# Squares of x one pair to a step, B's rows loaded from another place, and norm's splits in two parts

## The chip, the cores and the metric

The kernel runs on one core of one Trainium2 chip. The metric is the device time of an execution in microseconds (us); a smaller time is better. Five engines work in parallel, each on a queue of its own: TensorE (PE in the profile; its weight loads are listed apart as PEld), VectorE (DVE), ScalarE (ACT), GpSimd (POOL) and SyncE (SP), which here only issues DMA transfers.

## What is computed

One inference step of a hybrid decoder layer for 256 prompt tokens and 8 x 8 sample tokens, 320 tokens in all, with a model width of 2048. Cut to what matters here:

```python
h = rms_norm(x, norm_mix_pre)
proj = h @ w_in                                   # u, v, z, (x, B, C), dt
# head group 1: gated MLP over chunks of 128 tokens
v = layer_norm(gelu(a_v))
gate_out = gelu(a_u) * (tril(w_s) @ v + b_s)
# head group 2: SSD
xbc = silu(causal_depthwise_conv(xbc))
y, state = ssd_scan(xs, softplus(dt_raw + bias), -exp(a_log), B, C, state)
y = (y + d_skip * xs) * silu(z)
y = y * rsqrt(mean(y * y, per group of 512) + EPS) * norm_w
x = x + rms_norm(concat(gate_out, y) @ w_out, norm_mix_post)
# then the feed-forward part
x = x + rms_norm(conv_ffn(rms_norm(x, norm_ffn_pre)), norm_ffn_post)
```

For the samples the SSD part keeps one state of 64 x 128 for each head and each of the 8 sequences; every new state is the old one times a decay, plus an outer product of x and B.

## The kernel before

The activations are held transposed: 128 features on the partitions, and 320 tokens in a row. All large products are made in three parts, so that they come close to fp32. Each weight slab is loaded by SP into a tile `wraw`, rounded by ACT into `whi` (line 123), and what is left over is formed by DVE as `wlo` (line 124). PE then makes hi x hi, hi x lo and lo x hi (lines 134 to 136), 128 x 128 weights by 320 tokens each. Three buffers of each of the three tiles turn over, so a load waits until the slab three places earlier has been split, and a split waits until PE has used the slab three places earlier.

**The order of the work** is fixed when the kernel is built. Each engine gets one queue; the order in it comes from priorities (mostly the order in which the program text runs, with weight slabs and the blocks marked `first()` ahead of it), and `tc.issue_after(i)` puts an instruction behind instruction `i` on the same engine. Work between the large products is written as generators: `bg` is a list that is worked off from its head, `side` a list whose members all move on. `tick()`, called between slabs, lets them advance; `yield 24, 0` says that the next step is due after 24 more matmuls.

**The first pass over v** (lines 688 to 719) is a loop over the 16 blocks `kt` of the 2048 input features. Each step splits one block of x into hi and lo (`x_ready`, with ACT's part kept in `x_split`), and multiplies 768 columns of v's weights, 18 matmuls to a step. Beside it stand `x_squares` (squares of two blocks on ACT, line 631, an addition on DVE, line 633), `dt_columns` (the weights of dt, loaded into a `wraw` buffer and scaled into `w_dt` by DVE, line 492), `dt_products`, and `root`, which sums the squares over the features by four small matmuls and makes their reciprocal root `r` with eleven small DVE operations (`rsqrt_of`). `with_r1` then spreads `r` over the partitions with three PE transposes (line 300), at the first `tick` of the next projection.

**The gate part** is a loop over four groups `g`. It projects u for the next group (`gate_up`, whose results pass through buffers `pv`, four of them, and a Gelu on ACT), mixes v for this group (`gate_mix`, loads by POOL), and multiplies by w_out (`chunk_out`).

**The SSD part** begins with copies of B by token. B was written earlier, row by row, into a DRAM tile `b_d`. For the prompt the rows are read back by POOL while the gate part runs. For the samples two tiles `b4` are loaded by SP at the begin of this part (line 856), each of them 32 rows repeated four times; `b_of_samples` (lines 858 to 863) rounds them on ACT and forms the low part of half the partitions on DVE. `ssd(g)` is a generator in `bg`: it loads states (lines 869 and 898), multiplies them with C (`yo_ps`, line 973), and then goes through 13 numbered steps, in which `shrinks`, `picks`, `ends` and `heads` say what is done when. `shrunk` multiplies a state by its decay on POOL (line 984). `heads_in` makes the convolution input of a group and `conv_proj` its convolution (DVE, line 462), `heads_out` the z projection; its `norm` (lines 1151 to 1161) is a generator in `side`: partial sums of squares, then the root and the scaling of four blocks of y (line 1160), each split into `ohi` (ACT, line 402) and `olo` (DVE, line 403) for `chunk_out`.

Of the kernel before, what the change touches and what calls it, by code (L numbers as in the profile page):

```python
# [8 lines left out]
F32 = mybir.dt.float32  # L9
# [3 lines left out]
ALU = mybir.AluOpType  # L13
# [3 lines left out]
P = 128  # L17
NP = 256
NB, TS = 8, 8
NS = NB * TS  # L20
NT = NP + NS
# [12 lines left out]
def hybrid_step(  # L34
# [10 lines left out]
    act, dve, pool, pe, sp = nc.scalar, nc.vector, nc.gpsimd, nc.tensor, nc.sync  # L45
# [6 lines left out]
    tp = ctx.enter_context(tc.tile_pool(name="tp", bufs=2))  # L52
# [46 lines left out]
    def col(i):  # L99
        return prm[:, i:i + 1]  # L100


    def first():

        return tc.high_priority(offset=200000)
# [25 lines left out]
    def accumulate(ps, w, xhi, xlo, first, last):  # L131
        whi, wlo = w
        made_so_far[0] += 3
        pe.matmul(ps, whi, xhi, start=first, stop=False)  # L134
        pe.matmul(ps, whi, xlo, start=False, stop=False)  # L135
        last_made[0] = pe.matmul(ps, wlo, xhi, start=False, stop=last).ins  # L136
        return last_made[0]

    def rows_of(w, k0, nk, c0, n):
        return w[k0 * P:(k0 + nk) * P, c0:c0 + n].rearrange("(k p) n -> p k n", p=P)  # L140
# [6 lines left out]
    def advance(tasks, task):  # L147

        try:
            need = next(task) or (0, 0)  # L150
            due[task] = made_so_far[0] + need[0], need[1]
            return True
        except StopIteration:
            tasks.remove(task)
            return False
# [13 lines left out]
    def finish(task):  # L169
        while task in side:  # L170
            advance(side, task)
        while task in bg:
            advance(bg, bg[0])
# [187 lines left out]
    b_d = dr.tile([NT, 512], F32, name="b_d")  # L361
# [34 lines left out]
    def split(hi, lo, x, scale=None):  # L396

        if scale is None:
            act.copy(hi, x)
            made = dve.tensor_tensor(out=lo, in0=x, in1=hi.bitcast(F32), op=ALU.subtract)  # L400
        else:
            high.append(act.activation(hi, x, AF.Copy, scale=scale).ins)
            made = dve.scalar_tensor_tensor(out=lo, in0=x, scalar=scale, in1=hi.bitcast(F32), op0=ALU.mult, op1=ALU.subtract)

        return made.ins
# [20 lines left out]
    def in_order(ap):  # L426

        return ap.rearrange("p (i j f) -> p j i f", j=4, f=32)
# [6 lines left out]
    with ExitStack() as mctx:  # L435
        op = mctx.enter_context(tc.tile_pool(name="op", bufs=1))
# [155 lines left out]
        with tc.tile_pool(name="gp", bufs=1) as gp:  # L592
# [21 lines left out]
            x_split = []  # L614
# [13 lines left out]
            def x_squares(kt):  # L628

                sq = acc[:, kt:kt + 2, :]  # L630
                act.activation(sq, xf[:, kt:kt + 2, :], AF.Square)
                if kt:
                    dve.tensor_tensor(out=acc[:, 0:2, :], in0=acc[:, 0:2, :], in1=sq, op=ALU.add)
# [54 lines left out]
            for kt in range(KD):  # L688
                x_ready(kt, 1)
                x = [h[:, kt, :] for h in hT]  # L690
                if kt < 4:
                    for g in range(2):
                        wb = slab(rows_of(w_in, kt, 1, V0 + 384 * g, 384), g, begins=kt + g == 0)
                        if kt == 0:
                            made_so_far[0] += 9
                            for i in (0, 2, 1):
                                for j in range(3):
                                    pe.matmul(ps[3 * g + j][:, :NT], wb(0, j)[i // 2], x[i % 2], start=i == 0, stop=False)
                        else:
                            for j in range(3):  # L700
                                accumulate(ps[3 * g + j][:, :NT], wb(0, j), *x, False, False)
                else:
                    wb = slab(rows_of(w_in, kt, 1, V0, 768))
                    for j in range(6):
                        accumulate(ps[j][:, :NT], wb(0, j), *x, False, kt == KD - 1)
                if 3 <= kt < 11:
                    x_squares(2 * (kt - 3))
                if kt in (5, 8):
                    dt_columns(kt // 8)
                if kt == 12:  # L710
                    r = root()
                if kt == 13:
                    dt_products()
                if kt == 14:

                    with tc.issue_after(rounded[0]):
                        act.activation(held, ones[:, 0:1], AF.Gelu)
# [57 lines left out]
            def gate_up(g):  # L775
                uf = gp.tile([P, 4, NT], F32, tag="vf", name="uf", bufs=2)
                project(w_in, U0 + 512 * g, lambda j, ps: scaled(ps, AF.Gelu, uf[:, j, :]))
                return uf
# [52 lines left out]
            for g in range(4):  # L831
                res = []
                mix = gate_mix(g, uf, res)
                bg.append(mix)
                if g < 3:
                    uf = gate_up(g + 1)
                    finish(mix)
                    chunk_out(w_out, g, *res, g == 0)
            finish(mix)
# [3 lines left out]
        with tc.tile_pool(name="sd", bufs=1) as sd:  # L843
            btok = sd.tile([P, 2, 512], F32, name="btok")

            bsp = sd.tile([P, 2, 512], F32R, name="bsp")
# [3 lines left out]
            pool.tensor_copy(cb[NS:, NT:], ident[NS:, NS:])  # L850
            for c in range(2):
                act.copy(btok[:, c].rearrange("p (j i f) -> p j i f", j=4, f=32), in_order(b_raw[:, 512 * c:512 * c + 512]))
            b4 = [sd.tile([P, 512], F32, tag=tag, name="b4", bufs=n) for tag, n in (("s1", 1), ("xde", 2))]
            for i in range(2):
                o = NP + 32 * i
                sp.dma_start(b4[i], b_d[o:o + 32].unsqueeze(0).broadcast_to([4, 32, 512]))

            def b_of_samples():
                for i in range(2):
                    act.copy(bsp[:, i].rearrange("p (j i f) -> p j i f", j=4, f=32), in_order(b4[i]))  # L860
                    for rs in (slice(32, 64), slice(96, P)):
                        h = bsp[rs, i].rearrange("p (j i f) -> p j i f", j=4, f=32)
                        dve.tensor_tensor(out=h, in0=in_order(b4[i][rs]), in1=h.bitcast(F32), op=ALU.subtract)

            def load_state(g, i):

# [13 lines left out]
            def ssd(g):  # L880
# [63 lines left out]
                for r in range(2):  # L944
# [3 lines left out]
                                  in0=ps[:, :NP].rearrange("p (c t) -> p c t", c=2),  # L948
                                  in1=upper.unsqueeze(1).to_broadcast([P, 2, P]), op=ALU.mult)
                dve.tensor_tensor(out=cb[NS:, :NS], in0=ps[NS:, NP:NT], in1=upper_s[NS:], op=ALU.mult)  # L950
                dve.tensor_tensor(out=cb[:NS, NT:], in0=ps[:NS, NP:NT], in1=upper_s[:NS], op=ALU.mult)
                for hb in range(2):
                    dve.tensor_tensor(out=cms[:, 4 * hb:4 * hb + 4], in0=cmask[:, 4 * hb:4 * hb + 4],
                                      in1=cT[:, g, NP + 32 * hb:NP + 32 * hb + 32].unsqueeze(1).to_broadcast([P, 4, 32]),
                                      op=ALU.mult)
# [60 lines left out]
                s1 = sd.tile([P, 512], F32, tag="s1", name="s1", bufs=1)  # L1016
# [49 lines left out]
                                             op0=ALU.mult, op1=ALU.add)  # L1066
                ends = {2: 0, 5: 1, 7: 2, 10: 3}
                picks = {0: (0, 1), 2: (2,), 5: (3,)}
                shrinks = {0: 0, 3: 1, 5: 2, 8: 3}
                e = 1 if g == 3 else 0  # L1070
                heads = {0: 0, 1: 1, 3: 2, 4: 3, 5: 4, 7: 5, 9 - e: 6, 10 - e: 7}
                states = {4: (g, 3), 7: (g + 1, 0), 9: (g + 1, 1), 12: (g + 1, 2)}
# [1 line left out]
                for n in range(13 - e):  # L1074
# [23 lines left out]
                    if n < 12 - e:  # L1098
# [4 lines left out]
                                   in1=dec[:, 2, h0:h0 + 8].unsqueeze(2).to_broadcast([P, 8, 64]), op=ALU.mult)  # L1103
# [19 lines left out]
            def final(g):  # L1123
# [7 lines left out]
                yield  # L1131

            tasks = [ssd(g) for g in range(4)]
            res = [[] for _ in range(4)]

            def heads_out(g):

                ssq = hp.tile([P, NT], F32, tag="ssq", name="ssq")
                y = x_of.pop(g)

                def z_evac(j, ps):
                    while y_made.get(g, -1) < j:
                        advance(bg, bg[0])
                    zs = tp.tile([P, NT], F32, tag="ev", name="zs", bufs=2)
                    with first():
                        scaled(ps, AF.Silu, zs)
                        dve.tensor_tensor(out=y[:, j, :], in0=y[:, j, :], in1=zs, op=ALU.mult)
                        add_square(ssq, y[:, j, :], j == 0, dve)
                project(w_in, Z0 + 512 * g, z_evac)

                def norm():
                    yield 24, 0
                    small = partial_sums(ssq, ssq_d[g])
                    yield 24, 0
                    rb = tp.tile([P, NT], F32, tag="pv", name="rb", bufs=4)
                    root_by_vector(small, ssq_d[g], 1.0 / 512, rb)

                    res[g] += [h[:, KD - 4:] for h in hT] if g == 3 else out_parts(hp, "o")
                    for j in range(4):
                        dve.tensor_tensor(out=y[:, j, :], in0=y[:, j, :], in1=rb, op=ALU.mult)  # L1160
                        split(res[g][0][:, j, :], res[g][1][:, j, :], y[:, j, :], col(prm_at["norm"][3] + 4 * g + j))
                task = norm()
                side.append(task)
                return task
# [97 lines left out]
    with tc.tile_pool(name="fp", bufs=1) as fp:  # L1262
# [157 lines left out]
        for k in BY_POOL:  # L1420
            f = acc[:, k, :]
# [111 lines left out]
```

## Time and profile before

| | us |
|---|---|
| median of 3 runs | 1766.85 |
| the three runs | 1763.17, 1766.85, 2859.62 |
| profiled execution | 1763.86 |
| its span | 1762.2 |

The span is divided by the profile into busy and idle time of each engine. A line of a timeline gives the start in us, the duration in us, the engine, the line of the kernel, the operation, the tiles written and read, their shapes and a count; in brackets stands how long the engine was idle before it, and what ended that. A line of a table by stretches gives the busy time of PE, PEld, DVE, ACT and POOL in the stretch with the number of instructions that began in it, then the granted clock of TensorE, the share of DMA time and GB/s. A line of waits says who waited for whom, in total, how often, and at most. Times of matmuls are modelled at their end.

| part | about us in the span |
|---|---|
| first pass over v | 5 to 54 |
| rest of v, B, C and the first heads, gate part | 54 to 424 |
| SSD part with its projections | 424 to 810 |
| feed-forward part | 812 to 1747 |

### The profile page before, as it was taken

The page shows a single profiled execution, that of the slowest core. Times are in us where ns is not written, and L with a number is a line of the kernel's source. Part 1 is how long each engine was busy: PE and PEld are TensorE (multiplying, and loading weights), DVE is VectorE, ACT ScalarE, POOL GpSimd, SP SyncE. Part 2 cuts the span into 40 slices and gives each one's busy share as a digit, 9 for nine tenths or more (in the row PEclk, how much of TensorE's full clock was granted, in tenths as well). Part 3 has the DMA queues.
Part 4 walks back from the last instruction along what each step waited for, and adds up shares of the span by engine and source line. Part 5 has one row for each costly group of instructions (what it writes and reads, how often), then busy time and mean ns, then how long its engine had stood idle before and what let it go on. Part 6 is the DMA issues. An engine that isn't in the chain of part 4 may idle for free.

```text
span 1762.2 us, 31244 instructions
## 1 busy us (share of the span) xinstructions
PE 1751.7 (99%) x12129; PEld 1730.0 (98%) x12129; DVE 1170.2 (66%) x2000; ACT 826.8 (47%) x1216; POOL 321.8 (18%) x683
## 2 busy tenths in 40 slices
PE   9999999999999999999999999999999999999998
PEld 9999999999999999999999999999999999999998
DVE  6548863656869787788855565665657565656575
ACT  6344545333656575645545434343434343333445
POOL 2432330000314323012211101010202010101004
PEclk9999999999999999999999999999999999999999
DMA  7786654445676766665654444545454545454542
GB/s 238 225 239 185 181 175 151 151 154 151 221 217 190 226 213 201 208 207 164 178 154 153 150 153 151 154 149 154 149 155 148 155 148 152 151 155 146 155 150 105
DMA packets 228796, 302.25 MB, mean 172 GB/s; under 512 B 20904, under 2 KB 153896, under 8 KB 228456
## 3 DMA queue, kind: packets, MB, share of 16 engines
q1 hardware_dynamic: 213752, 274.61, 51.4%
q0 software_dynamic: 5312, 12.26, 2.3%
q10 hardware_dynamic: 9584, 13.38, 2.1%
q8 instruction: 96, 1.57, 0.4%
q14 instruction: 52, 0.43, 0.1%
HBM read 280.51 MB, written 19.69 MB: 170 GB/s over the span
## 4 chain that ended last, share of the span: by engine, by line
PE 90%; DVE 4%; DMA 3%; issue 1%; ACT 1%; POOL 1%; SPq 0%; ACTq 0%; POOLq 0%; DVEq 0%
PE ps L134 18%; PE ps L135 18%; PE ps L136 18%; PE pd L134 10%; PE pd L135 10%; PE pd L136 10%; DVE wlo L124 1%; DMA wraw<-in_w_in 1%; PE y_ps L1054 1%; DMA st<-in_state_ssm 1%; DMA wraw<-in_ffn_w_up 1%; ACT whi L123 0%; PE sg L801 0%; PE up_ps L990 0%; POOL st L984 0%
## 5 line engine op out<-in xcount | busy, mean ns | idle before, releaser
L124 DVE TENSOR_TENSOR wlo<-wraw,whi 128x1024 fp32r<-128x1024 f32 (+2 forms) x480 | 581.9, 1213 | 420.6 <-ACT whi L123 418.7
L123 ACT CAST whi<-wraw 128x1024 fp32r<-128x1024 f32 (+2 forms) x479 | 495.7, 1035 | 664.3 <-PE ps L135 376.6
L134 PE MATMUL ps<-h_hi,whi 128*128 128x320 f32 x2428 | 751.0, 310 | 0.9 <-ACT whi L123 0.8
L136 PE MATMUL ps<-h_hi,wlo 128*128 128x320 f32 x2428 | 748.6, 309 | 0.7 <-DVE wlo L124 0.7
L135 PE MATMUL ps<-h_lo,whi 128*128 128x320 f32 x2428 | 749.1, 309 | 0.0
L134 PEld LDWEIGHTS ps<-h_hi,whi 128*128 128x128 f32 x2428 | 456.2, 188 | 4.2 <-issue 1.2
L136 PEld LDWEIGHTS ps<-h_hi,wlo 128*128 128x128 f32 x2428 | 456.3, 188 | 1.0 <-DVE wlo L124 1.0
L135 PEld LDWEIGHTS ps<-h_lo,whi 128*128 128x128 f32 x2428 | 456.5, 188 | 0.4
L136 PE MATMUL pd<-fhi,wlo 128*128 128x320 f32 x704 | 217.0, 308 | 0.0
L134 PE MATMUL pd<-fhi,whi 128*128 128x320 f32 x704 | 217.0, 308 | 0.0
L135 PE MATMUL pd<-flo,whi 128*128 128x320 f32 x704 | 217.0, 308 | 0.0
L134 PE MATMUL pd<-ohi,whi 128*128 128x320 f32 x448 | 138.9, 310 | 0.5 <-DVE pad L456 0.5
L136 PE MATMUL pd<-ohi,wlo 128*128 128x320 f32 x448 | 138.3, 309 | 0.0
L135 PE MATMUL pd<-olo,whi 128*128 128x320 f32 x448 | 138.3, 309 | 0.0
L134 PEld LDWEIGHTS pd<-fhi,whi 128*128 128x128 f32 x704 | 132.2, 188 | 0.0
L135 PEld LDWEIGHTS pd<-flo,whi 128*128 128x128 f32 x704 | 132.2, 188 | 0.0
L136 PEld LDWEIGHTS pd<-fhi,wlo 128*128 128x128 f32 x704 | 132.2, 188 | 0.0
L1298 POOL COPY ptf<-pad 128x2 f32<-128x2 f32 x88 | 21.1, 240 | 599.5 <-DVE pad L1286 599.0
L247 DVE TENSOR_TENSOR acc_ffn<-acc_ffn,pd 128x320 f32<-128x320 f32 (+1 forms) x161 | 77.4, 481 | 37.7 <-PE pd L136 36.3
L134 PEld LDWEIGHTS pd<-ohi,whi 128*128 128x128 f32 x448 | 84.1, 188 | 1.6 <-PE pd L136 0.9
L135 PEld LDWEIGHTS pd<-olo,whi 128*128 128x128 f32 x448 | 84.1, 188 | 0.3
L136 PEld LDWEIGHTS pd<-ohi,wlo 128*128 128x128 f32 x448 | 84.1, 188 | 0.0
(338 smaller groups left out, 1751.3 us busy)
## 6 DMA issues: line engine op xcount, KB each, us to landing
wraw<-in_ffn_w_up SPq DMA_DIRECT2D x176, 512.0 KB, 3.6
wraw<-in_w_in SPq DMA_DIRECT2D x132, 512.0 KB, 3.8
wraw<-in_ffn_w_down SPq DMA_DIRECT2D x88, 512.0 KB, 3.3
wraw<-in_w_out SPq DMA_DIRECT2D x64, 512.0 KB, 3.4
st<-in_state_ssm SPq DMA_DIRECT2D x40, 256.0 KB, 4.6
out_ssm_state_sample<-st ACTq DMA_DIRECT2D x30, 256.0 KB, 3.1
cs<-dacs_d SPq DMA_DIRECT2D x16, 320.0 KB, 5.0
wraw<-in_w_in SPq DMA_DIRECT2D x12, 384.0 KB, 4.0
```

Of the source, the lines that this page charges most:

```text
L123: rounded[:] = [act.copy(hi, raw).ins]
L124: dve.tensor_tensor(out=lo, in0=raw, in1=hi.bitcast(F32), op=ALU.subtract)
L134: pe.matmul(ps, whi, xhi, start=first, stop=False)
L135: pe.matmul(ps, whi, xlo, start=False, stop=False)
L136: last_made[0] = pe.matmul(ps, wlo, xhi, start=False, stop=last).ins
L247: added_last[:] = [dve.tensor_tensor(out=acc[:, nb, ts], in0=acc[:, nb, ts], in1=ps[:, ts], op=ALU.add).ins]
L1054: pe.matmul(ps[64 * i:64 * i + 64, cols], w(hl), x(hl, m, cpx), tile_position=(0, 64 * i), **flags)
L1298: pool.tensor_copy(ptf[:, k, :], pad[:, 256:258])
```

## The change

The squares of x begin at step 6 of the first pass instead of step 3, still one pair to a step, and on ACT they are put behind the split of that step's block of x. The root moves from step 12 to step 15, the last. B's rows for the samples are loaded within the gate part's loop, when the last projection of u has been written out (`g == 2`), into the four buffers `pv`, in halves of 256 columns, by POOL; `b_of_samples` works on these halves, with four copies and eight subtractions in place of two and four. The second state of each group is shrunk at step 2 instead of 3. `norm` yields after the second of its four blocks, so that the other two are due 24 matmuls later.

```diff
-                if 3 <= kt < 11:
-                    x_squares(2 * (kt - 3))
+                if 6 <= kt < 14:
+                    with tc.issue_after(x_split[-1]):
+                        x_squares(2 * (kt - 6))
                 if kt in (5, 8):
                     dt_columns(kt // 8)
-                if kt == 12:
+                if kt == 15:
                     r = root()
...
                 if g < 3:
                     uf = gate_up(g + 1)
+                    if g == 2:
+                        b4 = [[tp.tile([P, NT], F32, tag="pv", name="b4", bufs=4)[:, :256] for _ in range(2)] for _ in range(2)]
+                        for i in range(2):
+                            o = NP + 32 * i
+                            for h in range(2):
+                                pool.dma_start(b4[i][h], b_d[o:o + 32, 256 * h:256 * h + 256].unsqueeze(0).broadcast_to([4, 32, 256]))
                     finish(mix)
...
-            b4 = [sd.tile([P, 512], F32, tag=tag, name="b4", bufs=n) for tag, n in (("s1", 1), ("xde", 2))]
-            for i in range(2):
-                o = NP + 32 * i
-                sp.dma_start(b4[i], b_d[o:o + 32].unsqueeze(0).broadcast_to([4, 32, 512]))
-
             def b_of_samples():
                 for i in range(2):
-                    act.copy(bsp[:, i].rearrange("p (j i f) -> p j i f", j=4, f=32), in_order(b4[i]))
-                    for rs in (slice(32, 64), slice(96, P)):
-                        h = bsp[rs, i].rearrange("p (j i f) -> p j i f", j=4, f=32)
-                        dve.tensor_tensor(out=h, in0=in_order(b4[i][rs]), in1=h.bitcast(F32), op=ALU.subtract)
+                    for h in range(2):
+                        out = bsp[:, i].rearrange("p (j i f) -> p j i f", j=4, f=32)[:, :, 2 * h:2 * h + 2]
+                        raw = in_order(b4[i][h])
+                        act.copy(out, raw)
+                        for rs in (slice(32, 64), slice(96, P)):
+                            dve.tensor_tensor(out=out[rs], in0=raw[rs], in1=out[rs].bitcast(F32), op=ALU.subtract)
...
-                shrinks = {0: 0, 3: 1, 5: 2, 8: 3}
+                shrinks = {0: 0, 2: 1, 5: 2, 8: 3}
...
                         split(res[g][0][:, j, :], res[g][1][:, j, :], y[:, j, :], col(prm_at["norm"][3] + 4 * g + j))
+                        if j == 1:
+                            yield 24, 0
```

## The prediction

> **What bounds the kernel.** I read the page's first part, then TensorE's busy time by stretches, then the timeline of each engine in the stretches that fell short.
>
> ```profile
> span 1762.2 us, 31244 instructions
> ...
> PE 1751.7 (99%) x12129; PEld 1730.0 (98%) x12129; DVE 1170.2 (66%) x2000; ACT 826.8 (47%) x1216; POOL 321.8 (18%) x683
> ```
>
> TensorE (PE) is busy for all but 10.5 us of the span, and the change takes no matmul away. So it can only win back time in which PE stands still, and there is little of it. Stretches of 10 us show where:
>
> ```profile
> 20.00:30.00 10.00, 9.73 (x64) 9.03 (x63) 7.29 (x11) 8.35 (x14) 0.00 (x0) 1.00 0.74 211
> 30.00:40.00 10.00, 8.98 (x62) 8.72 (x61) 9.25 (x15) 6.09 (x10) 3.00 (x4) 1.00 0.62 168
> 60.00:70.00 10.00, 10.00 (x70) 10.00 (x69) 3.18 (x4) 3.16 (x3) 4.25 (x10) 1.00 0.94 294
> 430.00:440.00 10.00, 8.53 (x56) 8.00 (x56) 3.84 (x5) 3.13 (x4) 0.00 (x0) 1.00 0.79 188
> 440.00:450.00 10.00, 9.94 (x71) 7.74 (x70) 5.99 (x8) 5.70 (x9) 3.81 (x4) 0.83 0.99 312
> ```
>
> A stretch without a stall (60 to 70) starts 70 matmuls, one per 0.145 us or so; the number in brackets is more honest than the busy time, because the modelled end of a matmul (0.31 us after its start) covers a short stall. From 20 to 40 us 6 + 8 = 14 matmuls are missing, 2.0 us. From 430 to 440 another 14 are missing, and behind them the granted clock falls to 0.83. These two places are the ones that the change edits: the squares of x, and B's rows for the samples.
>
> **The squares and the root.** In the first pass over v, PE spends 18 matmuls (2.6 us) on each slab of weights. The timelines of PE, DVE and ACT at the eighth and ninth step:
>
> ```profile
> 27.78 0.31 PE L135 MATMUL ps_v<-h_lo,whi 128*128 128x320 f32 x1
> 28.27 0.41 PE L136 MATMUL ps_v<-h_hi,wlo 128*128 128x320 f32 x1 [0.18 <-DVE wlo L124]
> ...
> 30.87 0.31 PE L135 MATMUL ps_v<-h_lo,whi 128*128 128x320 f32 x1
> 32.20 0.41 PE L136 MATMUL ps_v<-h_hi,wlo 128*128 128x320 f32 x1 [1.02 <-DVE wlo L124]
> ```
> ```profile
> 26.93 0.42 DVE L492 TENSOR_TENSOR w_dt<-wraw_dt,vt 128x256 f32<-128x256 f32 x1 [1.33 <-DMA wraw_dt<-in_w_in]
> 27.27 0.95 DVE L124 TENSOR_TENSOR wlo<-wraw,whi 128x768 fp32r<-128x768 f32 x1
> 28.14 0.55 DVE L622 SCALAR_TENSOR_TENSOR h_lo<-vt,h_hi 128x320 fp32r<-128x320 f32 x1
> 28.60 2.67 DVE L633 TENSOR_TENSOR acc_mix<-acc_mix 128x640 f32<-128x640 f32 x3
> 31.19 0.95 DVE L124 TENSOR_TENSOR wlo<-wraw,whi 128x768 fp32r<-128x768 f32 x1
> ```
> ```profile
> 28.46 0.83 ACT L123 CAST whi<-wraw 128x768 fp32r<-128x768 f32 x1 [1.34 <-DMA wraw<-in_w_in]
> ```
>
> At 30.87 PE stops for 32.20 - 30.87 - 0.145 = 1.2 us, and the first matmul after it adds 0.1. It waits for wlo, which DVE could have begun at 29.3, when ACT's whi was there; three additions of squares stood before it. With one pair to a step only one of them (2.67 / 3 = 0.9 us) lies there: 28.6 + 0.9 + 0.95 = 30.45, before PE asks at 31.0. This stall goes: 1.3 us.
>
> The stall at 27.78 (0.35 us, 0.1 with the restart) has another cause: wlo stood behind w_dt, and w_dt behind the load of the dt columns, an order that the change does not touch. The smaller stalls before it (2.0 less 1.3 less 0.45, so 0.2 to 0.3 us) may go, but then PE only arrives earlier at the same load. I count nothing for either; if wlo comes to stand ahead of w_dt, the pass yields 2.0 instead of 1.3. DVE's step is then wlo, h_lo and one addition, 0.95 + 0.55 + 0.9 = 2.4 us of 2.6: tight, which is the cover that the new place has. Squares and additions themselves are only moved (eight and seven as before).
>
> The root moves from step 12 to 15. Its matmuls (the same number) then end the pass, and its eleven small DVE operations come behind the last matmul of v, where before they had ended with some 9 us to spare before PE needs their result, the spread of r:
>
> ```profile
> 48.09 0.16 DVE L265 SCALAR_TENSOR_TENSOR rs_r<-rs_t,rs_r 128x3 f32<-128x3 f32 x1
> ...
> 54.38 2.32 DVE L124 TENSOR_TENSOR wlo<-wraw,whi 128x1024 fp32r<-128x1024 f32 x2
> ```
> ```profile
> 57.26 0.49 PE L300 MATMUL spread<-ident,rs_r 128*128 128x128 f32 x3
> ```
>
> Eleven at 0.16 plus small gaps are 2 us. Put before the two wlo they are done at 56.4, 0.9 us early; put behind them (54.38 + 2.32 + 2 = 58.7), PE waits 1.4 us. The first is my value (no cost), because those two wlo belong to slabs that PE takes up only after the spread; the second is a bound.
>
> **B's rows.** The next rows are ACT's and PE's when the SSD part begins.
>
> ```profile
> 435.89 0.62 ACT L860 CAST bsp<-b 128x512 fp32r<-128x512 f32 x1 [4.22 <-DMA b<-b_d]
> 436.41 1.99 ACT L123 CAST whi<-wraw 128x1024 fp32r<-128x1024 f32 x2
> ```
> ```profile
> 436.42 0.31 PE L136 MATMUL ps<-h_hi,wlo 128*128 128x320 f32 x1
> 437.50 0.42 PE L134 MATMUL ps<-h_hi,whi 128*128 128x320 f32 x1 [0.78 <-ACT whi L123]
> 437.76 0.31 PE L135 MATMUL ps<-h_lo,whi 128*128 128x320 f32 x1
> 438.77 0.41 PE L136 MATMUL ps<-h_hi,wlo 128*128 128x320 f32 x1 [0.70 <-DVE wlo L124]
> ...
> 440.08 0.47 PE L135 MATMUL ps<-h_lo,whi 128*128 128x320 f32 x1
> ...
> 443.28 0.36 PE L135 MATMUL ps<-h_lo,whi 128*128 128x320 f32 x1
> ```
>
> ACT's queue is in order: the rounding of a weight slab stood for 4.2 us behind a copy that waited for B's rows. PE lost 0.93 and 0.86 us, 0.2 more in the two matmuls behind the gaps, and then ran 12 matmuls in 443.28 - 440.08 = 3.2 us, where 12 x 0.145 = 1.74 would do: 1.45 us of slow clock. Together 3.4 us. With the rows loaded after the last gate projection the copy waits for nothing. ACT pays four copies for two and DVE eight subtractions for four; DVE is busy 3.84 us of the 10 there and ACT 3.13, so that hides.
>
> On POOL the four new loads stand in a queue that is otherwise empty:
>
> ```profile
> 428.26 1.04 POOL L912 TENSOR_TENSOR xde<-xdt,dec 128x512 f32<-128x512 f32 x1 [49.58 <-ACT x L432]
> ```
>
> They wait until ACT has emptied the four buffers "pv", which they take over, and nothing is queued behind them for tens of us; the next to need a "pv" is the first z projection, long after the copies. What is late next is the state loads:
>
> ```profile
> PEld yo_ps L973 <- DMA st<-in_state_ssm: 0.5, 1, 0.5
> ```
> ```profile
> st<-in_state_ssm SPq DMA_DIRECT2D x8, 256.0 KB, 10.7
> ```
>
> PE waits 0.5 us for them now, landing 10.7 us after issue, and it will arrive 3.4 us earlier. SP's issues come earlier too, since they wait for weight buffers that DVE frees sooner, and two loads of 256 KB leave this stretch. So between nothing and 2 us is given back, 2 if the landing moves by no more than 1.4 us; I take 0.5. The term is 2.9.
>
> **Norm's splits and the earlier shrink.** Nothing is added, the order changes. Half of the four multiplications and four subtractions may run 24 matmuls (3.5 us) later.
>
> ```profile
> 551.44 1.93 DVE L403 SCALAR_TENSOR_TENSOR olo<-xs,prm,ohi 128x320 fp32r<-128x320 f32 x4
> ...
> 558.81 2.02 DVE L462 SCALAR_TENSOR_TENSOR cv<-pad,prm,cv 128x344 f32<-128x344 f32 x4
> ```
> ```profile
> 555.62 0.31 PE L134 MATMUL pd<-ohi,whi 128*128 128x320 f32 x1
> ```
>
> The last low part is there at 553.4; PE needs it at the eleventh matmul from 555.62, at 557.1. 3.7 us of room against 3.5: no cost, no gain, and it is the tightest cover of the change. The shrink is POOL work a step sooner, ahead of its use; nothing.
>
> **Sum.** 1.3 + 2.9 = 4.2 us. The profiled execution took 1763.86 us (span 1762.2 and 1.7 around it), 3 us under the median of the runs, which holds 1763.17, 1766.85 and one of 2859.62. 1763.86 - 4.2 = 1759.7; I say **1760**.
>
> **Rivals.** (1) *The additions bunch still.* The diff orders ACT's squares behind the split of x, not DVE's additions. Against it: an addition follows its square. Then the 1.3 us stay: 1761. (2) *The root comes late*, behind the two wlo: 1.4 us at the spread, and a slow stretch of 1.45 like the one at 440: 1763. (3) *The state loads take the place of B's rows*, 2 us instead of 0.5: 1761. (4) *The slow clock does not hang on that stall.* The window from 30 to 40 has a stall of 1.2 us with the clock at 1.00, the one at 436 two of 0.9; only the second was followed by a slow stretch, so a cause beside the stall is not excluded. Then 1.45 us stay: 1761. The Trainium skill ("TensorE: Matmul & The Clock Gate", Part 1) speaks for it: the clock halves after about 3.4 us of idle window, more than PE's two gaps together. (5) *Slower: norm's second half falls behind the convolution work of the next heads.* For the first two groups that is twelve operations of L462 (2.02 / 4 each), 6 us, and four operations of its own at 0.48 (1.93 / 4), 1.9; less the 3.7 of room PE stands 4 us, and with a slow stretch 5.5, twice: 11 - 4.2, so 1771. It decides from 557.1 on. For it: the wait of 24 matmuls is nearly all the room. Against it: the half is issued two ticks before the convolutions' results exist.
>
> **How the numbers follow.** Forecast 0.62, rivals (1) 0.10, (2) 0.10, (3) 0.06, (4) 0.05, (5) 0.07. The range runs from 1755, all stalls won (2.0 + 3.4 + 0.5 off 1763.2, and a little of the same spread again), to 1768: rivals 1 to 4 and an execution 3 to 4 us up, as 1766.85 stands to 1763.17. It leaves out (5). About 2% (35 us) is what a measurement of this kernel can tell from no change. PE's idle 10.5 us bound any gain far below that, and even (5) twice over for all four groups stays within: same 0.97, faster 0.01, slower 0.02, the last for an order of instructions that I do not foresee.
>
> **What would show it.** The 20 to 40 stretch should start some 9 matmuls more, with wlo never behind two additions; the casts of B's rows should show no wait for a DMA, PE should stand at most 0.5 us between 430 and 450, and the clock there should be 1.00. The spread should follow the matmul before it without a gap, and the first matmul on ohi the last projection's. A gap at the spread, at the state products or at the first column of an output chunk would make it wrong, and a span over 1762 would say that the stalls only moved.

## The result, and the profile after

The changed kernel took 1759.41 us, the median of 9 runs (1757.36 to 1760.76); the kernel before took 1764.58 us beside it. The ratio is 0.9971 with a 95% interval of 0.9961 to 0.9982: 5.2 us less, faster by 0.3%, and within 2%. Forecast were 1760 in a range of 1755 to 1768, and 4.2 us less. One run of the kernel before took 2859.62 us and is left out of the comparison.

The first part of the page after:

```profile
span 1757.5 us, 31257 instructions
PE 1748.8 (100%) x12129; PEld 1727.8 (98%) x12129; DVE 1171.2 (67%) x2004; ACT 826.8 (47%) x1218; POOL 325.5 (19%) x687
```

PE still does its 12129 matmuls; the time that it was not busy fell from 10.5 to 8.7 us. The stretches of 10 us that the prediction looked at, after the change:

```profile
20.00:30.00 10.00, 9.25 (x60) 8.47 (x59) 6.67 (x11) 6.48 (x11) 0.00 (x0) 1.00 0.71 197
30.00:40.00 10.00, 10.00 (x70) 10.00 (x69) 9.76 (x16) 7.76 (x13) 3.43 (x4) 1.00 0.75 218
60.00:70.00 10.00, 10.00 (x70) 10.00 (x70) 4.05 (x4) 3.32 (x4) 4.66 (x11) 1.00 0.96 285
430.00:440.00 10.00, 10.00 (x71) 9.99 (x70) 6.13 (x9) 5.75 (x10) 0.69 (x1) 1.00 0.92 309
440.00:450.00 10.00, 10.00 (x86) 8.32 (x85) 9.51 (x15) 6.30 (x15) 7.80 (x8) 1.00 0.54 165
```

From 430 to 450 nothing is missing any more and the clock is 1.00. From 30 to 40 the 62 matmuls have become a full 70, but from 20 to 30 there are 60 in place of 64. VectorE's and PE's timelines of the first pass after the change:

```profile
27.56 0.43 DVE L492 TENSOR_TENSOR w_dt<-wraw_dt,vt 128x256 f32<-128x256 f32 x1 [1.31 <-DMA wraw_dt<-in_w_in]
27.90 0.95 DVE L124 TENSOR_TENSOR wlo<-wraw,whi 128x768 fp32r<-128x768 f32 x1
28.77 0.55 DVE L622 SCALAR_TENSOR_TENSOR h_lo<-vt,h_hi 128x320 fp32r<-128x320 f32 x1
29.23 0.82 DVE L633 TENSOR_TENSOR acc_mix<-acc_mix 128x640 f32<-128x640 f32 x1
29.97 0.95 DVE L124 TENSOR_TENSOR wlo<-wraw,whi 128x768 fp32r<-128x768 f32 x1
```
```profile
22.30 0.31 PE L135 MATMUL ps_v<-h_lo,whi 128*128 128x320 f32 x1
23.04 0.41 PE L136 MATMUL ps_v<-h_hi,wlo 128*128 128x320 f32 x1 [0.43 <-DVE wlo L124]
...
28.28 0.31 PE L135 MATMUL ps_v<-h_lo,whi 128*128 128x320 f32 x1
28.91 0.42 PE L136 MATMUL ps_v<-h_hi,wlo 128*128 128x320 f32 x1 [0.32 <-DVE wlo L124]
```

There is one addition between two low parts now, and PE no longer stands at the ninth step. But the wait behind dt's load, 0.35 us before, is 28.91 - 28.28 - 0.15 = 0.48, and there is a wait of 0.59 at 22.30 that the profile of before lacks. That second wait is not the change's doing: e2 and e3, two runs below that keep the old squares, have it too (0.59 and 0.60). It differs from execution to execution (0.25 in e12, which is the same kernel as after). PE in e2:

```profile
22.87 0.41 PE L136 MATMUL ps_v<-h_hi,wlo 128*128 128x320 f32 x1 [0.43 <-DVE wlo L124]
```

At B's rows, the queue of ACT and the first products with the states (PE):

```profile
427.68 1.32 ACT L865 CAST bsp<-b 128x256 fp32r<-128x256 f32 x4
429.23 1.05 ACT L123 CAST whi<-wraw 128x1024 fp32r<-128x1024 f32 x1 [0.22 <-ACT bsp L865]
```
```profile
441.51 1.93 PE L977 MATMUL yo_ps<-st,cb_cms 128*32 128x256 f32 x32
```

The four copies wait for no DMA, and neither does the slab behind them. The 32 products with states took 1.93 us in one piece.

To compare runs I use two landmarks on PE: the first product of C and B (`cb_ps`), where the gate part is over, and the start of the second block of products with the scores (`y_ps`; its first block starts 24 us earlier) some 80 us later. In after they are these rows:

```profile
424.70 0.61 PE L946 MATMUL cb_ps<-cT,bT 128*128 128x128 f32 x4
...
503.63 0.66 PE L1058 MATMUL y_ps<-cs,xdt 128*64 128x128 f32 x8
```

| profiled run | to `cb_ps` | `cb_ps` to `y_ps` | `y_ps` to end | median time |
|---|---|---|---|---|
| before | 425.10 | 83.59 | 1253.5 | 1764.58 |
| after | 424.70 | 78.93 | 1253.9 | 1759.41 |
| e1 squares and root | 425.26 | 83.42 | 1254.7 | 1763.75 |
| e2 rows | 425.93 | 79.07 | 1254.7 | 1762.08 |
| e3 norm and shrink | 426.62 | 82.49 | 1255.9 | 1764.47 |
| e4 dt scaled later | 424.79 | 79.55 | 1256.6 | 1761.10 |
| e5 squares and rows | 424.72 | 78.93 | 1257.1 | 1759.34 |
| e6 dt in own tiles | 424.70 | 78.93 | 1254.5 | 1760.30 |
| e7 no last shrink | 424.43 | 78.93 | 1253.7 | 1758.80 |
| e8 rows by SP | 424.53 | 79.48 | 1254.5 | 1760.20 |
| e9 squares late, unbound | 424.87 | 79.07 | 1255.2 | 1762.03 |
| e10 dt loads later | 422.30 | 79.07 | 1255.8 | 1758.61 |
| e11 the same, old squares | 423.15 | 79.08 | 1255.9 | 1759.01 |
| e12 changed again | 424.68 | 78.93 | 1253.0 | 1759.71 |

The columns are us of one profiled execution each. The kernel before took 1764.68 beside e1 to e4, 1764.59 beside e5 to e8, 1765.48 beside e9 and e10, 1764.22 beside e11 and e12.

### The profile page after: what moved, and what is told of

Same layout as the page of the kernel before. It is cut to its first block, busy times and chain, and to the rows that moved or that the text cites. A ratio compares the mean times of both kernels' runs of the same rounds, so it can differ in the third digit from the quotient of the medians.

```text
span 1757.5 us, 31257 instructions
## 1 busy us (share of the span) xinstructions
PE 1748.8 (100%) x12129; PEld 1727.8 (98%) x12129; DVE 1171.2 (67%) x2004; ACT 826.8 (47%) x1218; POOL 325.5 (19%) x687
## 4 chain that ended last, share of the span: by engine, by line
PE 60%; DVE 0%; issue 0%; ACT 0%; ACTq 0%
PE ps L134 13%; PE ps L136 12%; PE ps L135 12%; PE pd L135 7%; PE pd L136 7%; PE pd L134 7%; PE x1p L1402 0%; PE fin_ps L1130 0%; PE y_ps L1058 0%; PE tsum L292 0%; PE ps_other L136 0%; PE ps_other L134 0%; PE ps_other L135 0%; PE ps L188 0%; PE yo_ps L977 0%; PE up_ps L994 0%
```

## The experiments

### The three parts alone (e1, e2, e3)

e1 has the first two edits of the change and the old loads of B's rows:

```diff
+                if 6 <= kt < 14:
+                    with tc.issue_after(x_split[-1]):
+                        x_squares(2 * (kt - 6))
...
+                if kt == 15:
                     r = root()
```

> Kernel before with the squares and the root moved, nothing else. Theory as predicted (the additions of squares on DVE cost the first pass 1.3 us): 1.0 to 1.6 us under before, no wait at the ninth step's first wlo, the wait for the dt columns' load at the eighth step of 0.4 to 0.6 us still there. Rival (the pass is paced by its loads: a stall that DVE no longer makes is made by a slab or by the dt columns arriving late): 0 to 0.6 us under before. In both, the stall at B's rows (two gaps of about 0.9 us) and the slow clock behind it stay.

1763.75, ratio 0.9995 (0.9986 to 1.0004): 0.9 us less, with zero inside the interval. In e1's profile PE no longer stands at the ninth step, but it stands 29.47 - 28.30 - 0.15 = 1.02 us behind dt's load, where 0.4 to 0.6 were expected. e2 has B's rows alone:

```diff
+                                pool.dma_start(b4[i][h], b_d[o:o + 32, 256 * h:256 * h + 256].unsqueeze(0).broadcast_to([4, 32, 256]))
...
-                sp.dma_start(b4[i], b_d[o:o + 32].unsqueeze(0).broadcast_to([4, 32, 512]))
```

> Kernel before with B's rows loaded behind the last gate projection by POOL, nothing else. Theory (ACT's copies of B's rows held up the rounding of a weight slab): 3.4 to 4.2 us under before, no wait of ACT for B's rows, granted clock 1.00 from 430 to 450, state products of 1.9 us instead of 2.6. Rival, the state loads take over: 1.4 to 2 us under before, with a wait at the state products of 2 us. Rival, the slow clock does not hang on the stall: 2 us under before, with the clock at about 0.83 there.

1762.08, ratio 0.9985 (0.9976 to 0.9994): 2.6 us less. Its stretch from `cb_ps` to `y_ps` is 4.5 us shorter than before's. Of that its profile lost 0.8 up to `cb_ps`, 0.59 of it in the wait near 22, and 1.2 behind `y_ps`, where PE stood 0.5 us for a `pad` near 552. e3 has norm's two parts and the shrink:

```diff
-                shrinks = {0: 0, 3: 1, 5: 2, 8: 3}
+                shrinks = {0: 0, 2: 1, 5: 2, 8: 3}
...
+                        if j == 1:
+                            yield 24, 0
```

> Kernel before with norm's splits in two parts and the second state's shrink one step sooner, nothing else. Theory (order only, covered by 3.7 us of room): within 0.5 us of before. Rival (the second half falls behind the convolution): 3 to 11 us over before, with PE waiting for olo at the first column of an output chunk.

1764.47, ratio 0.9995 (0.9986 to 1.0004). Here there is a plainer answer than a time: the built queue of every engine holds the same instructions in the same order with these lines as without them. The two edits change when a generator may go on, but no instruction passes another. So e3 is a second look at the kernel before, and a useful one, as is e1 at the place of B's rows. PE at B's rows and its stretch from 440 to 450, in e1 and then in e3:

```profile
437.86 0.41 PE L134 MATMUL ps<-h_hi,whi 128*128 128x320 f32 x1 [0.97 <-ACT whi L123]
439.12 0.41 PE L136 MATMUL ps<-h_hi,wlo 128*128 128x320 f32 x1 [0.70 <-DVE wlo L124]
...
440.00:450.00 10.00, 8.35 (x71) 6.16 (x70) 5.78 (x7) 4.57 (x7) 4.98 (x5) 1.00 0.96 298
```
```profile
439.48 0.42 PE L136 MATMUL ps<-h_hi,wlo 128*128 128x320 f32 x1 [0.70 <-DVE wlo L124]
...
440.00:450.00 10.00, 8.38 (x71) 6.19 (x70) 6.09 (x8) 4.18 (x5) 4.63 (x5) 1.00 0.94 279
```

e1 has both stalls at B's rows, the first a little longer than before's; e3, whose ACT waited 3.73 us for the rows instead of 4.22, has only the second. In both the clock is 1.00 where before's was 0.83, and yet the same 71 matmuls begin. What PE does not lose to the clock it loses a moment later to the states, here in e1:

```profile
447.84 0.63 PE L974 MATMUL yo_ps<-st,cb_cms 128*32 128x256 f32 x6 [1.65 <-DMA st<-in_state_ssm]
```

In e3 the same wait is 1.62 us, and the stretch from `cb_ps` to `y_ps` took 83.42 us in e1 against before's 83.59. So the 1.45 us of slow clock were not a loss of their own: they covered a wait for a load that ends when it ends. Why that load is late, SP's queue tells, before and then after:

```profile
427.08 2.87 SPq L869 DMA_DIRECT2D st<-in_state_ssm  x5
438.74 0.38 SPq L117 DMA_DIRECT2D wraw<-in_w_in  x1
439.16 0.51 SPq L869 DMA_DIRECT2D st<-in_state_ssm  x1
```
```profile
424.59 0.82 SPq L873 DMA_DIRECT2D st<-in_state_ssm  x2
426.69 1.92 SPq L873 DMA_DIRECT2D st<-in_state_ssm  x4
431.64 0.38 SPq L117 DMA_DIRECT2D wraw<-in_w_in  x1
```

Before, the sixth state was issued at 439.16, behind a slab's load that waited for a buffer, which DVE could not free since ACT stood before B's rows. In e1 that issue came at 439.52 and in e3 at 439.87, and each time PE went on with the last state 8.3 us later. After, all six are issued by 428.6.

### Both parts that move instructions, and the change again (e5, e12)

```diff
-                shrinks = {0: 0, 2: 1, 5: 2, 8: 3}
+                shrinks = {0: 0, 3: 1, 5: 2, 8: 3}
...
-                        if j == 1:
-                            yield 24, 0
```

> The squares, the root and B's rows as in the changed kernel, without norm's two parts and with the second shrink at step 3 as before. The instructions of PE, ACT, POOL, SP and DVE then stand in the same order as in the changed kernel. Theory (norm and shrink change no queue, so they are worth nothing): 3.5 to 5.5 us under the kernel before, near 1759.4. Rival (norm's two parts or the earlier shrink are worth what the two halves alone leave open, 5.2 - 0.9 - 2.6 = 1.7 us): 1761.1.

1759.34, ratio 0.9973 (0.9963 to 0.9983), which is after's. The third part is worth nothing.

> The changed kernel once more, on the chip of the run beside it. Theory (the later loads of dt are worth 0.8 us or more in the time): 1 us or more above that run's sort, 5.2 us under the kernel before. Rival (the difference lies between the chips and calls): within 0.5 us of it.

1759.71, ratio 0.9973 (0.9962 to 0.9985), 0.7 us above its neighbour e11; that is between what the two theories expected and settles neither. The change itself came out as it did the first time.

### What makes the additions bunch (e9)

```diff
                 if 6 <= kt < 14:
-                    with tc.issue_after(x_split[-1]):
-                        x_squares(2 * (kt - 6))
+                    x_squares(2 * (kt - 6))
```

> B's rows as in the changed kernel; the squares of x begin at step 6 and the root stands at step 15, but ACT's squares are not put behind the split of x. In the built queues three additions of squares then stand together again ahead of a slab's low part, as in the kernel before, and the small operations of the root stand behind two low parts. Theory (the bunch of three additions is what costs, the place of the root nothing): TensorE stands 1.0 to 1.2 us for the low part of the ninth step, the first product of C and B begins near 425.9 as in the runs with the old order of squares, and the time is that of B's rows alone, 1762.1, within 0.8. Rival (the later begin of the squares is what counts, not the bunch): no stall of over 0.6 us, 1759.4.

1762.03, ratio 0.9981 (0.9972 to 0.9990), with the stall as expected. DVE and PE in e9:

```profile
28.08 2.68 DVE L633 TENSOR_TENSOR acc_mix<-acc_mix 128x640 f32<-128x640 f32 x3
30.67 0.95 DVE L124 TENSOR_TENSOR wlo<-wraw,whi 128x768 fp32r<-128x768 f32 x1
```
```profile
31.68 0.42 PE L136 MATMUL ps_v<-h_hi,wlo 128*128 128x320 f32 x1 [1.02 <-DVE wlo L124]
```

Without the binding the built queue holds the same bunch of three as before, though the squares are begun three steps later. The landmark missed its expectation: `cb_ps` came at 424.87 and not 425.9. In this execution PE's first product began at 4.95 instead of 5.42, which may be why. The binding alone, at the old steps, was not run, and need not be: its built queues are those of e2.

### What paces the first pass (e4, e6, e10, e11)

In e4 each block of dt is scaled one step later, behind that step's low part:

```diff
                 if kt in (5, 8):
-                    dt_columns(kt // 8)
+                    dt_raw = dt_columns(kt // 8)
+                if kt in (6, 9):
+                    with tc.issue_after(split_done[-1]):
+                        dt_scaled(*dt_raw)
```

> Changed kernel, with the scaling of each half of the dt columns put behind the next slab's split on DVE instead of ahead of the slab's. Theory (at the eighth step wlo stands behind w_dt, which waits for its load): that stall of 0.4 to 0.6 us goes, 0.5 us under the changed kernel, 5.5 to 6 us under before. Rival (the loads pace the pass): the buffer of the dt columns is held longer, the next slab's load starts later and the stall comes back one or two steps later: no difference from the changed kernel, 5 us under before.

1761.10, ratio 0.9974 (0.9964 to 0.9983). The stall at 28 went and came back as 0.51 at 31, as the rival had it. The time is worse than either expected: four of its ten runs lie near 1759.2, as the rival wanted, and the six others from 1760.8 to 1762.6. Its profile, one of the six, lost the difference behind 540, where PE stood 1.46 us for a `pad`; more on that place below. In e6 dt's weights get tiles of their own (two that are free until the end of the pass), so that they take no buffer from the slabs:

```diff
-                raw = wp.tile([P, 1024], F32, tag="wraw", name="wraw_dt", bufs=3)
+                raw = dt_raw[s]
...
+                if kt == 12:
+                    with tc.issue_after(split_done[-1]):
+                        dt_scaled(0)
+                        dt_scaled(1)
```

> The changed kernel, with the two blocks of dt's weights loaded into tiles of their own instead of the three buffers of the slabs, and scaled at step 12 of the first pass behind that step's split. Theory (the first pass is paced by the three buffers, of which dt's loads take one twice): the stalls of PE up to 60 us, 2.5 us in the changed kernel, fall to 1.2 or less, and the time is 1 to 1.5 us under the changed kernel, near 1758.2. Rival (the rate of the DMA paces it; the same bytes are loaded at the same place): the stalls only move, 2.5 us stay, and the time is that of the changed kernel, 1759.4.

1760.30, ratio 0.9977 (0.9968 to 0.9985); there are fewer stalls, as the theory of the buffers expected, but the time did not follow, and the theory fell. SP and PE in e6:

```profile
4.99 1.16 SPq L491 DMA_DIRECT2D turned<-in_w_in  x2
6.97 38.21 SPq L117 DMA_DIRECT2D wraw<-in_w_in  x16
```
```profile
15.12 0.41 PE L134 MATMUL ps_v<-h_hi,whi 128*128 128x320 f32 x1 [0.67 <-ACT whi L123]
```

With no buffer to wait for, both loads of dt went out at 4.99, ahead of the slabs, and PE stood at 15 instead of 22 and 28; `cb_ps` came at 424.70 as before. e10 issues the same two loads behind the slabs of steps 9 and 10; the four other engines' queues are those of e6:

```diff
-                if kt in (5, 8):
-                    dt_columns(kt // 8)
+                if kt in (9, 10):
+                    dt_columns(kt - 9)
```

> As the run with dt's weights in tiles of their own, but SP issues these two loads behind the slabs of steps 9 and 10 instead of behind the first six half slabs; the queues of the four other engines are the same. Theory (the rate of the DMA, 0.93 busy from 10 to 20 us, paces the first pass until step 9, and dt's 1 MB is part of what it carries there): no stall of over 0.3 us before 52 us, the first pass ends near 51, and the time is 1 to 1.5 us under the changed kernel, near 1758.2. Rival (the slabs and x alone fill the DMA's rate there): the stalls come back between 14 and 30 us, 1759.4 or more. Second rival (won here, lost to the stalls near 550 and 685 that differ from run to run): the first pass ends near 51, the time stays at 1759.4 to 1760.3.

1758.61, ratio 0.9960 (0.9948 to 0.9973). Its stretch from 20 to 30, and the end of the pass in e10 and then in after:

```profile
20.00:30.00 10.00, 10.00 (x71) 10.00 (x70) 9.31 (x14) 8.48 (x14) 0.00 (x0) 1.00 1.03 310
```
```profile
49.92 0.50 PE L644 MATMUL tsum<-ones,acc_mix 128*128 128x1 f32 x4
```
```profile
52.33 0.51 PE L640 MATMUL tsum<-ones,acc_mix 128*128 128x1 f32 x4
```

Where after moves 197 GB/s from 20 to 30, e10 moves 310, PE starts 71 matmuls instead of 60, and the pass ends 2.4 us earlier. The time lies between what the theory (1758.2) and the second rival (1759.4 or more) expected: from `y_ps` on, e10's profile lost 1.9 us to after's, and the intervals of the two ratios overlap. e10 has the lowest median of the kernels that compute everything; that it beats the change in time is likely but not settled.

e11 is e10 with the squares and the root of before (from step 3, unbound; step 12).

> As the run with dt's two loads behind the slabs of steps 9 and 10, but with the squares and the root where the kernel before has them (from step 3, not bound; root at step 12); B's rows stay moved. In the built queue DVE's additions then stand two together twice, never three. Theory (the bunch of three was a sequel of the slabs that came late; without it the old order costs nothing, so the squares' term and the loads' term are not to be added): no stall of over 0.3 us before 52 us, the first product of C and B near 422.3, and the time of the run that has both, 1758.6, within 0.7. Rival (two additions, 1.6 us, with wlo and h_lo, 0.95 + 0.55, are 3.1 us against a step of 2.6, so each pair costs a stall of 0.3 to 0.5): the first product of C and B near 423.1, the time 1759.4.

1759.01, ratio 0.9968 (0.9955 to 0.9980), and no stall over 0.15 us before 52 us. DVE in e11, where two additions now stand together:

```profile
24.72 1.75 DVE L637 TENSOR_TENSOR acc_mix<-acc_mix 128x640 f32<-128x640 f32 x2
26.39 0.95 DVE L124 TENSOR_TENSOR wlo<-wraw,whi 128x768 fp32r<-128x768 f32 x1
```

`cb_ps` came at 423.15, where the rival had put it, but without the rival's stalls: 0.85 after e10's and 1.5 before that of e12, which began as e11 did, at 5.42 with the first three matmuls in 1.15 us (e10's took 0.68). So with dt's loads later the old steps of the squares cost nothing that a trace shows. That the bunch of three is a sequel of dt's loads is not shown in full: the order in a queue is fixed when the kernel is built, and with these loads and their scaling moved it has pairs in place of the bunch. A bunch of three with slabs that are there in time was not run.

### B's rows on another queue (e8)

```diff
-                                pool.dma_start(b4[i][h], b_d[o:o + 32, 256 * h:256 * h + 256].unsqueeze(0).broadcast_to([4, 32, 256]))
+                                sp.dma_start(b4[i][h], b_d[o:o + 32, 256 * h:256 * h + 256].unsqueeze(0).broadcast_to([4, 32, 256]))
```

> The changed kernel, with B's rows loaded at the same place of the program but on SP's queue, where they stand behind five of the next output chunk's slabs, instead of on POOL's. Theory (what counts is that the rows are loaded before the SSD part begins): the copies of B's rows wait for no DMA, PE's stall from 430 to 450 stays under 0.5 us, the time is that of the changed kernel, 1759.4, within 1 us. Rival (POOL's empty queue is what the gain hangs on; on SP the waiting loads hold up the slabs behind them, each of which PE uses up in 2.6 us): a stall of 1 us or more before 425 or at the copies, 1761 or more.

1760.20, ratio 0.9974 (0.9965 to 0.9983); in e8, too, the four copies wait for nothing:

```profile
427.51 1.32 ACT L865 CAST bsp<-b 128x256 fp32r<-128x256 f32 x4
```

The place in time is what counts, not POOL's queue; `y_ps` came 0.55 us later behind `cb_ps` than in after.

### The stalls behind 540 (e7)

```diff
-                    if n in shrinks:
+                    if n in shrinks and (g, n) != (0, 8) and (g, n) != (1, 8):
```

> The changed kernel without the multiplication of the last state by its decay (step 8) in head groups 0 and 1, so those states are left without it. Theory (VectorE's low parts of the scaled y take 2.7 to 3.6 us instead of 1.9 where GpSimd's shrink begins in the middle of them): four low parts of group 0 take 1.93 us, PE stands at most 0.3 us before the output chunk near 550, and the time is between that of the changed kernel and 1.2 us under it. Rival (the low parts are slowed by something else, such as ACT's high parts): 2.7 us or more may still be seen, and a stall of 0.7 or more behind it.

1758.80 (1758.16 to 1759.40), ratio 0.9966 (0.9954 to 0.9978). e7 leaves the last state of these two groups without its decay, so it does not compute the layer; it only shows what this work costs where it stands. Two kernels with equal queues show what the last shrink does, in one profile each. GpSimd and VectorE in after; then GpSimd, VectorE and PE in e5:

```profile
547.17 3.59 POOL L988 TENSOR_TENSOR st<-st,tote 128x512 f32<-128x512 f32 x2 [13.66 <-DMA st<-in_state_ssm]
```
```profile
545.75 1.94 DVE L403 SCALAR_TENSOR_TENSOR olo<-xs,prm,ohi 128x320 fp32r<-128x320 f32 x4
547.60 1.22 DVE L124 TENSOR_TENSOR wlo<-wraw,whi 128x1024 fp32r<-128x1024 f32 x1
```
```profile
547.50 2.33 POOL L988 TENSOR_TENSOR st<-st,tote 128x512 f32<-128x512 f32 x2 [13.73 <-DMA st<-in_state_ssm]
```
```profile
546.16 2.75 DVE L403 SCALAR_TENSOR_TENSOR olo<-xs,prm,ohi 128x320 fp32r<-128x320 f32 x4
548.84 2.08 DVE L124 TENSOR_TENSOR wlo<-wraw,whi 128x1024 fp32r<-128x1024 f32 x1
```
```profile
551.53 0.39 PE L134 MATMUL pd<-ohi,whi 128*128 128x320 f32 x1 [1.12 <-DVE pad L456]
```

In after GpSimd got in during the last low part, was held up itself (3.59 us for two operations instead of 2.33), and DVE was not. In e5 it was DVE that waited, 0.8 us each in a low part and in a slab's low part (2.08 for 1.22), and PE stood 1.12 us for the `pad` behind them. A state's load (13.7 us of waiting) sets the moment, a few tenths of a us decide. In before, after, e6 and e12 DVE's four low parts took 1.9 us, in the nine other runs that have the shrink 2.7 to 3.6; from `y_ps` to the end the first four took 1253.0 to 1254.5, the nine 1254.5 to 1257.1 (in e3, e6 and e11 a stretch of half clock between 1744 and 1755 is in it as well). In e7 they took 1.9, with no stall for the `pad`, and its time lies 0.6 us under after's; the two intervals overlap.

## Why the prediction was right, and where its sizes were off

The forecast was the likeliest case, and the two parts it counted won: 5.2 us measured, 4.2 forecast. Its terms:

- **The squares, 1.3 forecast, about 0.9 measured.** To `cb_ps`, the runs with bunched additions (before, e2, e3, e9) took 425.63 in the mean, those with one addition to a step and dt as it was (after, e1, e5, e7, e8, e12) 424.72. The two groups overlap (424.87 to 426.62 and 424.43 to 425.26), and e1's time, 0.9 less, has zero inside its interval; e9, which lacks only the binding, has a ratio of 0.9981 against the change's 0.9971 and 0.9973, 1.4 to 1.8 us. So the size is rough. The stall that was named went as described. The likely reason for the smaller gain is the one that the prediction gave of the smaller stalls alone, "PE only arrives earlier at the same load", and did not apply to this one. It took the wait behind dt's load as fixed; that wait was 0.34 to 0.50 us in before, e2 and e3 and is 0.48 to 1.02 in the six others, 0.34 more in the mean. e10 and e11 show that with dt's loads out of the way both waits go, in e11 with the old steps of the squares.
- **Rival 1** was not the case, but its reason "an addition follows its square" is not what spreads the additions: e9 has the later squares and still the bunch. The binding together with the later steps does it: the binding alone leaves the queues as they were.
- **The root, nothing forecast, 0.24 us measured.** The prediction put the small operations ahead of the two low parts. They came behind them, the case that it priced at 1.4 (timeline of DVE after):

```profile
52.97 2.32 DVE L124 TENSOR_TENSOR wlo<-wraw,whi 128x1024 fp32r<-128x1024 f32 x2
55.21 0.15 DVE L259 TENSOR_SCALAR rs_v<-tsum 128x3 f32<-128x3 f32 x1
...
58.88 0.15 DVE L265 SCALAR_TENSOR_TENSOR rs_r<-rs_t,rs_r 128x3 f32<-128x3 f32 x1
```
```profile
58.80 0.31 PE L134 MATMUL ps<-h_hi,whi 128*128 128x320 f32 x1
59.19 0.51 PE L300 MATMUL spread<-ident,rs_r 128*128 128x128 f32 x3
```

  It cost 59.19 - 58.80 - 0.15 = 0.24 and not 1.4, because the spread moved too: in PE's built queue it stands behind 40 products of the next projection, before behind 24, and 16 x 0.147 = 2.35 us. The number was right for a reason that the prediction did not have; it held one queue fixed and moved the other.
- **B's rows, 2.9 forecast, 4.1 measured.** From `cb_ps` to `y_ps` the three runs with the old loads took 83.17 in the mean, the eleven others 79.09. The step that failed is the give-back of 0.5 us to the state loads (rival 3: 2 us): it had the wrong sign. Their late issue hung on the same stall, as SP's queue shows, and PE's wait for them, 2.61 - 1.93 = 0.68 us in before, went with it (3.4 + 0.7 = 4.1). In before's own profile the stretch shrank by more, 83.59 - 78.93 = 4.66, and no row names the rest. The products with the states in before:

```profile
445.45 2.61 PE L973 MATMUL yo_ps<-st,cb_cms 128*32 128x256 f32 x32
```

- **Rival 4** was neither right nor wrong: the slow stretch followed the two gaps in before and did not follow them in e1, where the states took its 1.45 us. That settles the sum, not the cause of the clock.
- **Norm and the shrink, nothing forecast, nothing measured.** "The order changes" was wrong: no queue changed. So rival 5 could not occur here; whether 24 matmuls of delay would cost what it says was not tried.
- **Of what should be seen**, 9 matmuls more from 20 to 40 were promised and 4 came (130 for 126). One low part, at 39.06, still stands behind two additions (0.82 and 0.49 us), without a stall of PE. The other marks held, but for the gap of 0.24 at the spread.

By these landmarks 0.9 and 4.1 make 5.0 of the 5.2. The times of the two parts alone, 0.9 (e1) and 2.6 (e2), make only 3.5; each is uncertain by over 1 us, and the profiles of e1 and e2 have GpSimd's last shrink in the way of VectorE's low parts, those of before and after do not, which no part of the change decides. The squares came out smaller and B's rows larger than forecast, which in part cancels, so the hit on the time is in part luck.

## What to carry to other kernels

A stall in a queue has followers on other queues: before pricing what comes next after it is gone, look whether the next wait was set by the same stall, as SP's sixth state load was. Where loads pace a stretch, a stall that is won in an instruction order can be lost again at the next load; move first what the loads need not carry there. And an edit to a generator's due times has an effect only if some engine's built queue differs.

## What the runs showed of the hardware

GpSimd's and VectorE's operations on SBUF held each other up by whole operations: low parts of 0.55 us became up to 1.38 us, and GpSimd's pair of 2.33 us became 3.59. The Trainium skill ("SBUF — State Buffer", section "SBUF: two separate sides") says that a VectorE operation with two SBUF inputs and a GpSimd operation that reads SBUF take one port pair as an exclusive lock, and that the one that starts first keeps it for its whole instruction. These traces agree in who waits: in e5 GpSimd's pair began at 547.50, just ahead of the last low part (547.55), and the low part lost 0.8 us; in after it began at 547.17, just behind the last low part (547.14), and GpSimd waited. They show more than one instruction's wait, though: in after GpSimd's first operation took 2.57 us, past that low part and past the slab's low part that followed it on VectorE at 547.60. That kernels with equal queues differ by over 1 us of 1760 through this (PE stood 1.12 us for the `pad` in e5, not at all in after) had not been expected.

The granted clock fell to 0.83 of the stretch after two gaps of 0.93 and 0.86 us in the profile of before; within it the clock was half, as a view of before shows:

```profile
440.00:443.30 3.30, 3.30 (x15) 3.30 (x14) 2.55 (x3) 1.84 (x3) 0.00 (x0) 0.50 0.94 309
```

It stayed at 1.00 after gaps of 1.13 and 0.86 us in e1, and after one of 0.86 in e3. In e3, e6 and e11 it was half for 3.4 us between 1744 and 1755, where the other profiles show none of it. The two gaps are 1.8 us together, less than the idle window of 3.4 us that the prediction went by; what else it takes stays open.
